# Weight preparation in a GLA slot loop: one piece a slot, or steps at eight places of the slot

## The chip, the cores and the metric

The program runs on 1 core of one Trainium2 chip. The core has five engines that work side by side: TensorE (PE in the profile, its weight loads PEld), VectorE (DVE), ScalarE (ACT), GpSimd (POOL) and SyncE (SP, which issues most of the DMAs). Each engine runs its instructions in the order in which they stand in its own queue, and waits in front of an instruction until what it needs is there. The metric is the device time of one execution in microseconds (us): 1320.1 us for the kernel before, the median of 3 runs (1319.07 to 1321.24).

## The reference

One step of a diffusion backbone with two layers. Layer 0 mixes tokens with gated linear attention (GLA), layer 1 with softmax attention. There are 256 context tokens and 1024 latent tokens of width 1024. The change touches layer 0 alone, of which this is what matters (chunks of 64 tokens, 4 heads, forward and backward in time):

```
proj = h @ w_in;  q, k, v, gate = split(proj)
logg = log_sigmoid((h @ wa1[d]) @ wa2[d] + ba[d]) / 16
for each chunk:  b = cumsum(logg);  qe = q*exp(b);  ke = k*exp(-b)
    a = tril(qe @ ke.T);  o = a @ v + qe @ S
    S = exp(b_last)*S + (k*exp(b_last - b)).T @ v
o = rms_norm(o_f + flip(o_b), onorm)
x = x + gt * ((o * silu(gate)) @ w_out)
```

The weights come in 32 bits. The kernel multiplies in 16 bits and keeps the accuracy by splitting every operand into a scaled high and a low half (three products for one).

## The kernel before

**Slots.** The GLA layer is one loop (`gla`) over 5 x 10 slots. A slot is one tile of 128 tokens of one head; there are 4 heads, and the fifth round only finishes the fourth head. In slot (h, n) the loop works on tile `order[n]`: `decayed` (L549) makes `en` and `qe` from the cumulated decay, `decay` (L525) prepares the decay of the slot after next, `value_gate` (L506) multiplies the tile with the value weights of head h and the gate weights of head h-1, `intra` (L567) makes the matrix `A` inside the tile (masked into `am` by VectorE, summed into `at` by GpSimd), `outer` (L587) and `scan` (L604) carry the state on in one direction (`Sa`, `Wa`), and `combine` (L642) and `gated` (L661) carry the other direction of the head before (`Sc`, `Wc`), add both and gate them. `local` (L628) multiplies `at` and `Sa` one slot later. So each slot is a chain that runs several times through TensorE, ScalarE, VectorE and GpSimd, and the large matrix products (L125) of `value_gate` and of the next head's q and k (`qk_piece`) stand between its links.

**Weight blocks.** A block is 1024 x 256 numbers of a weight matrix in 32 bits. `stage` (L138) loads it into one of two buffers `wst` (a DMA on SP's queue). Then a job splits it: `fill` (L179) for GLA weights, `fill_out` (L156) for the output weights, `split_ahead` (L191) for attention weights that go back to memory. A job is four reductions of 128x512 on VectorE (the block's largest value, L148 or L162), a small chain that makes a power of two of it, in which TensorE transposes once (`pow2`, L84), and four pairs of a scaled copy on ScalarE (L186, L175, L205) and a difference on VectorE (L187, L176, L206). `fold_gate` (L757) is eight multiplications of 128x256 on GpSimd (L762); it runs once, in the fifth round. The 16 matrices `wada` are loaded by SP too (L280) and used by `gemv` two slots later.

**Order.** The functions only record instructions. A scheduler then orders them for each engine, by the place where they were recorded, their dependencies and its own estimate of time; `issue_after(x)` keeps what is recorded under it behind instruction x on x's engine. In the kernel before, a staged block becomes an entry of `jobs`, and at one place of the next slot, behind `en` (`self.mark`), the whole job is recorded:

```
with self.tc.issue_after(self.mark):
    while self.jobs:
        run(self.jobs.pop(0))
```

The state of a latent sequence is loaded by SP (L614) into a single buffer `s0`, which also holds the last state on its way out (`final_state`, L624) and a row of `b_ada` (L313).

Of the kernel before, what the change touches and what calls it, by code (L numbers as in the profile page):

```python
# [52 lines left out]
class K:  # L53
# [84 lines left out]
    def stage(self, ap):  # L138
        st = self.t(self.wst, [P, KT, 256], F32, "wst")
        self.nc.sync.dma_start(st, ap.rearrange("(k p) n -> p k n", p=P))  # L140
        return st


    def scale(self, st):
        nc = self.nc
        mx = self.t(self.small, [P, 4], F32, "wmx")
        for j in range(4):
            nc.vector.tensor_reduce(  # L148
                mx[:, j : j + 1], st[:, 2 * j : 2 * j + 2, :], AX.XY, ALU.max, apply_absolute_value=True
            )  # L150
        m = self.t(self.small, [P, 1], F32, "wm1")
        nc.vector.tensor_reduce(m, mx, AX.X, ALU.max)
        return self.pow2(m)


    def fill_out(self, w, st):  # L156
        nc = self.nc
        mx = self.t(self.small, [P, 2, 2], F32, "wmx")
        par = st.rearrange("p (q b j) n -> p q b j n", q=2, j=2)
        for q in range(2):  # L160
            for b in range(2):
                nc.vector.tensor_reduce(  # L162
                    mx[:, q, b : b + 1], par[:, q, :, b, :], AX.XY, ALU.max, apply_absolute_value=True
                )
        o2 = self.onorm.unsqueeze(1).to_broadcast([P, 2, 2])
# [12 lines left out]

    def fill(self, w, j, st):  # L179
        nc = self.nc  # L180
        s, w[2][j] = self.scale(st)
        h = KT // 4
        for i in range(4):
            a, n = slice(i * h, i * h + h), slice(256 * j, 256 * j + 256)
            hi, lo = w[0][:, a, n], w[1][:, a, n]
            act = nc.scalar.activation(hi, st[:, a, :], AF.Copy, scale=s)  # L186
            dve = nc.vector.scalar_tensor_tensor(lo, st[:, a, :], s, hi, ALU.mult, ALU.subtract)  # L187
        return act.ins, dve.ins


    def split_ahead(self, name, j, st):  # L191
        nc = self.nc
        s, inv = self.scale(st)
# [6 lines left out]
        for i in range(2):  # L200
            a = slice(i * h, i * h + h)
            t = self.t(self.spl, [P, 2, h, 256], F16, "split")
            for b in range(0, h, 2):
                u, v = st[:, i * h + b : i * h + b + 2, :], slice(b, b + 2)
# [28 lines left out]
    def silu(self, x, n, tag="ls"):  # L233
# [3 lines left out]
        nc.vector.tensor_tensor(x, x, u, ALU.mult)  # L237
# [289 lines left out]
    def decay(self, h, i):  # L527
# [12 lines left out]
        nc.vector.scalar_tensor_tensor(g, u, G_SCALE, g, ALU.mult, ALU.add)  # L540
# [26 lines left out]
    def intra(self, i, st):  # L567
# [13 lines left out]
        nc.vector.copy_predicated(am, self.mask, ap)  # L581
# [21 lines left out]
    def scan(self, h, i, d, prev, u, eb, tag):  # L603
# [15 lines left out]
        if u is not None:  # L619
            w = self.t(self.ew, [P, DV], F32, "W" + tag)  # L620
            nc.vector.tensor_tensor(w, s, u, ALU.add)
# [37 lines left out]
    def gated(self, h, i, og, r, g):  # L659
        nc = self.nc  # L660
        nc.vector.scalar_tensor_tensor(g, og, r, g, ALU.mult, ALU.mult)  # L661
# [19 lines left out]
    def gla_init(self):  # L681
# [3 lines left out]
        self.v = [[None] * NT for _ in range(GH)]  # L685
        self.jobs = []

    def gla(self, wq, w, filler):
# [5 lines left out]
        for h in range(GH + 1):  # L694
# [8 lines left out]
            for n, i in enumerate(order):  # L703
# [37 lines left out]
                if h == 1 and n == 3:  # L741
                    self.fold_qk(1, wq)
# [3 lines left out]
            if h < GH:  # L746
                w = nw
# [8 lines left out]
    def fold_gate(self, gt, inv):  # L756
        nc = self.nc  # L757
        self.gt = gt
        for b in range(4):
            for i in range(2):  # L760
# [382 lines left out]
    def attention(self, wo, wk):  # L1143
# [45 lines left out]
        self.fold_gate(*self.gate_load(1), wo[0][2] + wo[1][2])  # L1189
# [49 lines left out]
def run(job):  # L1239
    return job[0](*job[1:])  # L1240
# [3 lines left out]
def emit(ctx, tc, I, O, dbg=None, stop=None):  # L1244
# [28 lines left out]
    with ExitStack() as c:  # L1273
# [98 lines left out]
        def filler(slot):  # L1372
# [30 lines left out]
            if slot == 40:  # L1403
                k.jobs.append((k.fold_gate, *k.gate_load(0), [t[2] for t in wo]))
# [6 lines left out]
            if slot in PREP:  # L1411
                n = PREP.index(slot)
                a = k.t(k.wst, [P, KT, 256], F32, "wst").rearrange("p k n -> p (k n)")[:, 0:D]
# [138 lines left out]
```

## Time and profile before

| what | value |
|---|---|
| runs of the kernel before | 1319.07, 1320.10, 1321.24 us |
| the profiled execution's own time | 1319.83 us |
| its span in the trace | 1318.1 us |
| TensorE busy | 1226.3 us (93%) |
| VectorE busy | 906.2 us (69%) |
| ScalarE busy | 713.5 us (54%) |
| GpSimd busy | 337.3 us (26%) |
| mean granted TensorE clock | 0.979 |

The slot loop lies between about 90 us and 560 us of the span: the first of its 40 rows `en` (L560) starts at 92.4 us, the last at 525.9 us, and the fifth round ends some 30 us later. After it come the output product of layer 0, layer 1 and its output. The profile shows how long each engine was busy and, for idle time, which other engine's instruction ended it. In a row of the timeline the numbers are the start, the time taken, the engine, the line, the operation and the tiles written and read, and at the end in brackets the idle time before it with what ended it.

### The profile page before, as it was taken

How to read it: one execution, taken by the hardware profiler on the slowest of the kernel's cores; microseconds unless marked ns; L12 is line 12 of the kernel's file. 1: busy time of each engine (PE TensorE's matmuls, PEld its weight loads, DVE VectorE, ACT ScalarE, POOL GpSimd, SP SyncE). 2: the span in 40 equal slices, each digit the busy share in tenths (PEclk: the TensorE clock that was granted, in tenths of full speed). 3: DMA queues.
4: the chain of work that ended last, by engine and by line, in shares of the span. 5: the costliest groups of instructions: out<-in, count | busy, mean ns of one | idle time of the engine just before them, and what ended most of it. 6: DMA issues, size and time to landing. Idle time of an engine off the chain costs nothing. (4 is left out here: it accounts for less than half of the span.)

```text
span 1318.1 us, 22427 instructions
## 1 busy us (share of the span) xinstructions
PE 1226.3 (93%) x8058; PEld 800.2 (61%) x8058; DVE 906.2 (69%) x2109; ACT 713.5 (54%) x1730; POOL 337.3 (26%) x575
## 2 busy tenths in 40 slices
PE   3799998999999998897999899999999999989997
PEld 1366665655555655674877567766665766756444
DVE  5676778776867788765765667677757677686552
ACT  2674546655656565642433476666767677673110
POOL 2132212322322243501222524232132244211000
PEclk8899998999999999998999899999999999999999
DMA  9712555545545534258444287676848748869432
GB/s 345 260 33 65 179 182 156 172 137 158 188 137 161 168 117 146 81 138 278 122 126 143 70 198 137 124 136 133 196 85 182 147 85 141 190 133 236 148 135 74
DMA packets 339487, 199.11 MB, mean 151 GB/s; under 512 B 229502, under 2 KB 325486, under 8 KB 337072
## 3 DMA queue, kind: packets, MB, share of 16 engines
q1 hardware_dynamic: 291328, 159.56, 47.4%
q10 hardware_dynamic: 47728, 37.36, 8.8%
q8 instruction: 63, 1.03, 0.3%
q0 software_dynamic: 320, 0.77, 0.3%
q14 instruction: 48, 0.39, 0.1%
HBM read 104.31 MB, written 37.24 MB: 107 GB/s over the span
## 5 line engine op out<-in xcount | busy, mean ns | idle before, releaser
L125 PEld LDWEIGHTS <-hT_hi 128*128 128x128 f16 x1920 | 189.0, 99 | 128.8 <-issue 16.3
L125 PE MATMUL mm<-whi,hT_hi 128*128 128x512 f16 (+1 forms) x576 | 200.8, 349 | 2.4 <-ACT gx L517 2.3
L125 PE MATMUL mm<-wlo,hT_hi 128*128 128x512 f16 (+1 forms) x576 | 200.7, 349 | 0.0
L125 PE MATMUL mm<-whi,hT_lo 128*128 128x512 f16 (+1 forms) x576 | 200.6, 348 | 0.0
L1085 DVE SCALAR_TENSOR_TENSOR phl<-p,srec,phl 128x1280 f16<-128x1280 f32 (+1 forms) x80 | 109.3, 1369 | 76.6 <-POOL phl L1082 43.4
L125 PEld LDWEIGHTS <-whi 128*128 128x128 f16 x1232 | 120.5, 98 | 62.8 <-issue 5.5
L125 PE MATMUL mm<-hT_hi,whi 128*128 128x256 f16 (+1 forms) x480 | 141.0, 294 | 1.9 <-DVE og L1110 1.4
L125 PE MATMUL mm<-hT_lo,whi 128*128 128x256 f16 (+1 forms) x480 | 141.0, 294 | 0.0
L125 PE MATMUL mm<-hT_hi,wlo 128*128 128x256 f16 (+1 forms) x480 | 141.0, 294 | 0.0
L125 PEld LDWEIGHTS <-hT_lo 128*128 128x128 f16 x960 | 94.4, 98 | 60.9 <-issue 2.1
L1052 PE MATMUL S<-kT,wst 128*128 128x512 f16 (+1 forms) x624 | 123.9, 341 | 7.2 <-ACT p L1060 7.2
L125 PE MATMUL mm<-PT,vh 128*128 128x256 f16 x672 | 113.8, 275 | 10.3 <-DMA PT<-phl 10.3
L1082 POOL TENSOR_SCALAR phl<-p,srec 128x1280 f16<-128x1280 f32 (+1 forms) x40 | 54.7, 1367 | 267.1 <-DVE srec L1076 132.4
L1055 DVE TENSOR_REDUCE smx<-S 128x1 f32<-128x1280 f32 (+1 forms) x80 | 101.5, 1269 | 7.6 <-PE S L1052 7.6
L1060 ACT ACTIVATE p<-S,snb,sexp 128x1280 f32<-128x1280 f32 (+1 forms) x80 | 99.3, 1242 | 7.6 <-DVE srec L1078 1.7
L1052 PEld LDWEIGHTS <-wst 128*128 128x128 f16 x624 | 61.4, 98 | 61.4 <-issue 10.3
L125 PE MATMUL mm<-PT,vl 128*128 128x256 f16 x336 | 92.3, 275 | 0.0
L148 DVE TENSOR_REDUCE wmx<-wst 128x1 f32<-128x512 f32 x104 | 64.5, 677 | 30.6 <-DMA wst<-in_gla_w_in 16.6
L125 PEld LDWEIGHTS <-vh 128*128 128x128 f16 x672 | 65.7, 99 | 21.0 <-issue 10.8
L125 PEld LDWEIGHTS <-wlo 128*128 128x128 f16 x616 | 60.3, 98 | 29.3 <-DVE wlo L1213 0.2
L1057 ACT ACTIVATE snb<-smx,nsexp 128x1 f32<-128x1 f32 x80 | 23.2, 290 | 85.4 <-DVE smx L1055 85.0
L892 POOL TENSOR_TENSOR rope<-hx,ropet 128x64 f32<-128x64 f32 x160 | 60.8, 409 | 20.3 <-ACT hx L1018 11.8
(357 smaller groups left out, 2706.0 us busy)
## 6 DMA issues: line engine op xcount, KB each, us to landing
wada<-in_w_ada SPq DMA_DIRECT2D x16, 1024.0 KB, 7.5
wst<-in_gla_w_in SPq DMA_DIRECT2D x12, 1024.0 KB, 6.4
wst<-in_att_w_in SPq DMA_DIRECT2D x10, 1024.0 KB, 7.4
og_d<-gx ACTq DMA_DIRECT2D x40, 128.0 KB, 1.8
og_d<-og ACTq DMA_DIRECT2D x40, 128.0 KB, 2.7
wst<-og_d SPq DMA_DIRECT2D x5, 1024.0 KB
xr<-x_d SPq DMA_DIRECT2D x9, 512.0 KB, 3.4
out<-xr ACTq DMA_DIRECT2D x17, 256.0 KB, 2.0
```

What stands on the lines that cost most here:

```text
L125: self.nc.tensor.matmul(out, a, b, start=k == 0 and j == 0, stop=k == n - 1 and j == 2)
L148: nc.vector.tensor_reduce(mx[:, j : j + 1], st[:, 2 * j : 2 * j + 2, :], AX.XY, ALU.max, apply_absolute_value=True)
L892: nc.gpsimd.tensor_tensor(tv[:, h, :, w, :], xv[:, h, :, 1 - w, :], sn[:, :, w, :], ALU.mult)
L1052: nc.tensor.matmul(S[:, a : a + n], x, y, start=m == 0, stop=m == 2)
L1055: last = nc.vector.tensor_reduce(mx, S, AX.X, ALU.max).ins
L1057: nc.scalar.activation(nb, mx, AF.Copy, scale=self.nsexp)
L1060: nc.scalar.activation(p, S, AF.Exp, scale=self.sexp, bias=nb, accum_out=den)
L1082: nc.gpsimd.tensor_scalar(hi, p, r, 2.0 ** 14, ALU.mult, ALU.mult)
L1085: nc.vector.scalar_tensor_tensor(lo, p, r2, hi, ALU.mult, ALU.subtract)
```

## The change

Jobs become generators: `scale`, `fill_out`, `fill`, `split_ahead` and `fold_gate` get a `yield` behind each reduction and ahead of each pair (or each pair of folds), nine steps for a block. `start` puts a job under way where it was recorded whole before. `step` records the next step of the oldest job under way, behind the chain's instruction just recorded on VectorE (`anchor`) and the TensorE instruction recorded last; it is called at eight places of a slot (five in the first round, four in the fifth). A step that needs TensorE's `pow2` waits for a place that allows it (`bank`). `room` finishes the oldest job in one piece where a buffer `wst` is needed, and `finish` all of them at a round's end and ahead of `fold_qk`.

```diff
     def stage(self, ap):
+        self.room(2)
         st = self.t(self.wst, [P, KT, 256], F32, "wst")
...
                 mx[:, j : j + 1], st[:, 2 * j : 2 * j + 2, :], AX.XY, ALU.max, apply_absolute_value=True
             )
+            yield j == 3
...
     def fill(self, w, j, st):
         nc = self.nc
-        s, w[2][j] = self.scale(st)
+        s, w[2][j] = yield from self.scale(st)
         h = KT // 4
         for i in range(4):
+            yield False
...
+    @contextmanager
+    def behind(self, ins):
+        if ins is None:
+            yield
+        else:
+            traced = self.nc.cur_bb.bb.instructions
+            pe = next(i for i in reversed(traced) if i.engine == mybir.EngineType.PE)
+            with self.tc.issue_after(ins), self.tc.issue_after(pe):
+                yield
+
+    def room(self, n):
+        with self.behind(self.mark):
+            while self.under and len(self.under) + len(self.jobs) >= n:
+                list(self.under.pop(0))
+                self.wants = None
+
+    def step(self, ins, bank=True):
+        while self.under and (bank or not self.wants):
+            with self.behind(ins):
+                self.wants = next(self.under[0], None)
+            if self.wants is not None:
+                return
+            self.under.pop(0)
...
                 if local:
                     self.local(*local)
                     local = None
+                    self.step(self.anchor)
                 if h < GH:
                     s = st[h][i] = self.decayed(h, i, g.pop(slot))
+                    self.step(self.mark, False)
                 h2, n2 = divmod(slot + 2, NT)
                 if h2 < GH:
                     g[slot + 2] = self.decay(h2, orders[h2][n2])
+                    self.step(self.anchor, False)
                 x = self.value_gate(h, i, w)
+                if h > 0:
+                    self.step(self.anchor, False)
                 if h < GH:
                     self.intra(i, s)
+                    self.step(self.anchor, h == 0)
                 if h > 0:
                     og, r, cprev = self.combine(h - 1, i, a, st[h - 1][i], cprev)
+                    self.step(self.mark if h == GH else self.anchor)
                     self.gated(h - 1, i, og, r, x)
+                    self.step(self.anchor)
...
                 with self.tc.issue_after(self.mark):
-                    while self.jobs:
-                        run(self.jobs.pop(0))
+                    self.start()
                 filler(slot)
                 if h < GH:
                     self.outer(h, i, a, s, prev, i in ends)
+                    self.step(self.anchor)
...
         for b in range(4):
+            if b:
+                yield False
             for i in range(2):
                 g = gt[:, i, 256 * b : 256 * b + 256]
                 nc.gpsimd.tensor_scalar(g, g, inv[b], 1.0, ALU.mult, ALU.mult)
```

Both programs hold the same instructions on every engine, in another order inside the loop; behind the loop the order is the same. In VectorE's order, 26 runs of four or more large rows of jobs (reductions and differences) stand unbroken in the loop before, and 16 now; rows of a job that stand alone between two rows of the chain were 11 and are 49.

VectorE, the third slot of the second round (slot 12), before. `Wc` and `Wa` are the two scans; `ks`, `g`, `ls`, `glo`, `gx` and `og` are links of the chain, `wm1` is the end of a block's maximum; `qe9` feeds TensorE's product `A` of this slot:

```order
L621 TENSOR_TENSOR Wc_598_2472<-Sc_596_2468,u9_418_1771 128x256
L152 TENSOR_REDUCE wm1_606_2492<-wmx_605_2487 128x1
L539 TENSOR_SCALAR g_627_2557<-z_625_2551,ninv_z_118_449 128x256
L229 SCALAR_TENSOR_TENSOR ls_591_2450<-gx_590_2448,ls_591_2450 128x256
L540 SCALAR_TENSOR_TENSOR g_627_2557<-ls_626_2553,g_627_2557 128x256
L621 TENSOR_TENSOR Wc_639_2613<-Sc_638_2611,u8_384_1655 128x256
L237 TENSOR_TENSOR gx_590_2448<-gx_590_2448,ls_591_2450 128x256
L621 TENSOR_TENSOR Wa_618_2531<-Sa_616_2527,U_615_2525 128x256
L545 TENSOR_TENSOR glo_629_2561<-g_627_2557,ghi_628_2560 128x256
L562 TENSOR_TENSOR qe9_581_2404<-ep_580_2401,q1_455_1923 128x256
```

VectorE at the same place now (`split` is a difference of a block, `modT1` belongs to the next layer's conditioning; the lines of the changed program are higher by 3 to 6 there):

```order
L627 TENSOR_TENSOR Wc_591_2450<-Sc_589_2446,u9_410_1744 128x256
L155 TENSOR_REDUCE wm1_598_2463<-wmx_570_2367 128x1
L212 SCALAR_TENSOR_TENSOR split_566_2351<-wst_465_1968,p2s_555_2318,split_566_2351 128x512
L580 COPY ks_628_2580<-kt_627_2577 128x256
L312 TENSOR_TENSOR modT1_39_174<-mm_646_2622,cT_34_159 128x4
L568 TENSOR_TENSOR qe9_574_2379<-ep_573_2376,q1_443_1881 128x256
L657 TENSOR_TENSOR og_593_2454<-o_592_2452,oa9_413_1752 128x256
L627 TENSOR_TENSOR Wc_632_2591<-Sc_631_2589,u8_373_1612 128x256
L545 TENSOR_SCALAR g_663_2673<-z_661_2667,ninv_z_118_449 128x256
L627 TENSOR_TENSOR Wa_610_2498<-Sa_608_2494,U_607_2492 128x256
```

Before, `Wc` and `Wa` of this slot both stand ahead of `qe9`; now only `Wc` does, and `Wa` stands four rows behind it. A block's differences, which ended ahead of `Wc`, now stand between the rows of the chain. On TensorE the product `o` that reads this `Sc` stood five large matmuls (L125, 128x512) ahead of `A` with `qe9`, and now stands 24 ahead of it.

SP's DMA queue at the same place, before (the two rows `s0` from `in_state_gla` are the loads that `Sc` and `Sa` of this slot read):

```order
L140 DMA wst_576_2388<-in_gla_w_in 128x8x256
L614 DMA s0_597_2469<-in_state_gla 128x256
L280 DMA wada_647_2632<-in_w_ada 128x8x256
L614 DMA s0_617_2528<-in_state_gla 128x256
L140 DMA wst_648_2634<-in_att_w_in 128x8x256
```

And now:

```order
L142 DMA wst_522_2211<-in_gla_w_in 128x8x256
L286 DMA wada_647_2626<-in_w_ada 128x8x256
L620 DMA s0_590_2447<-in_state_gla 128x256
L620 DMA s0_609_2495<-in_state_gla 128x256
L142 DMA wst_568_2361<-in_gla_w_in 128x8x256
```

The large load `wada` stood between the two small state loads and stands ahead of both now.

GpSimd in the last slots of the loop, before (`wst` in place is the gate's fold, `at` is the sum that `local` waits for, `ors` a small power, `Sa` and `Sc` links of the scans):

```order
L583 TENSOR_TENSOR at_6203<-am_31_149 128x128
L762 TENSOR_SCALAR wst_6554<-wst_6554,p2i_5455 128x256
L762 TENSOR_SCALAR wst_6554<-wst_6554,p2i_5755 128x256
L762 TENSOR_SCALAR wst_6554<-wst_6554,p2i_6240 128x256
L762 TENSOR_SCALAR wst_6554<-wst_6554,p2i_5455 128x256
L617 TENSOR_SCALAR Sa_6493<-Wa_6377,eb_1687_6301,eb_1715_6395 128x256
L762 TENSOR_SCALAR wst_6554<-wst_6554,p2i_5755 128x256
L762 TENSOR_SCALAR wst_6554<-wst_6554,p2i_6240 128x256
L116 TENSOR_TENSOR ors_6363<-orsa_6361,mhalf_81 128x1
L583 TENSOR_TENSOR at_6348<-am_30_148 128x128
```

And now:

```order
L589 TENSOR_TENSOR at_6323<-am_30_148 128x128
L623 TENSOR_SCALAR Sc_6595<-Wc_6539,eb_1715_6393,eb_1679_6274 128x256
L623 TENSOR_SCALAR Sc_6648<-Wc_6597,eb_1679_6274,eb_1636_6141 128x256
L117 TENSOR_TENSOR ors_6455<-orsa_6453,mhalf_81 128x1
L820 TENSOR_SCALAR wst_6554<-wst_6554,p2i_5572 128x256
L820 TENSOR_SCALAR wst_6554<-wst_6554,p2i_5863 128x256
L820 TENSOR_SCALAR wst_6554<-wst_6554,p2i_6353 128x256
L623 TENSOR_SCALAR Sc_6709<-Wc_6650,eb_1636_6141,eb_1597_6013 128x256
L589 TENSOR_TENSOR at_6442<-am_31_149 128x128
```

The last but one `at` stood behind six folds and the last behind all eight; now the last but one stands ahead of all of them, and the last behind three.

More of the change, by code (lines that the diff above doesn't have):

```diff
@@ L1 @@
-from contextlib import ExitStack
+import inspect
+from contextlib import ExitStack, contextmanager
 import concourse.bass as bass
@@ L180, in fill @@
         nc = self.nc
[L181 removed]
+        s, w[2][j] = yield from self.scale(st)
         h = KT // 4
         for i in range(4):
+            yield False
             a, n = slice(i * h, i * h + h), slice(256 * j, 256 * j + 256)
             hi, lo = w[0][:, a, n], w[1][:, a, n]
[L186 to L188 removed]
+            nc.scalar.activation(hi, st[:, a, :], AF.Copy, scale=s)
+            nc.vector.scalar_tensor_tensor(lo, st[:, a, :], s, hi, ALU.mult, ALU.subtract)
     def split_ahead(self, name, j, st):
         nc = self.nc
[L193 removed]
+        s, inv = yield from self.scale(st)
         h = KT // 2
@@ L685, in gla_init, with finish, start @@
         self.v = [[None] * NT for _ in range(GH)]
+        self.jobs, self.under, self.mark, self.wants = [], [], None, None
+    @contextmanager
[19 more added lines that the diff above has]
+            self.under.pop(0)
+    def finish(self):
+        with self.behind(self.mark):
+            for job in self.under:
+                list(job)
+        self.under, self.wants = [], None
+    def start(self):
+        for job in self.jobs:
+            r = job[0](*job[1:])
+            if inspect.isgenerator(r):
+                self.under.append(r)
         self.jobs = []
@@ L1188, in attention @@
                         self.prep = self.out2_prep(row, (first[:, 0], first[:, 1]))
-        self.fold_gate(*self.gate_load(1), wo[0][2] + wo[1][2])
+        run((self.fold_gate, *self.gate_load(1), wo[0][2] + wo[1][2]))
         wo[:] = [(hi, lo, 512) for hi, lo, _ in wo]
@@ L1239, in run @@
 def run(job):
-    return job[0](*job[1:])
+    r = job[0](*job[1:])
+    return list(r) if inspect.isgenerator(r) else r
 @with_exitstack
@@ L1403, in filler @@
             if slot == 40:
+                k.room(2)
                 k.jobs.append((k.fold_gate, *k.gate_load(0), [t[2] for t in wo]))
@@ L1412, in filler @@
                 n = PREP.index(slot)
+                k.room(1)
                 a = k.t(k.wst, [P, KT, 256], F32, "wst").rearrange("p k n -> p (k n)")[:, 0:D]
```

15 lines of the change are left out of this document (10 added, 5 removed).

## The prediction

> **What bounds the kernel now.** I read the page's first part, then the busy time by stage, then TensorE's waits in the loop, and only then the timelines around the longest of them.
>
> ```profile
> span 1318.1 us, 22427 instructions
> PE 1226.3 (93%) x8058; PEld 800.2 (61%) x8058; DVE 906.2 (69%) x2109; ACT 713.5 (54%) x1730; POOL 337.3 (26%) x575
> 90.00:560.00 470.00, 449.34 (x2774) 283.41 (x2772) 360.08 (x980) 272.70 (x715) 142.26 (x242) 0.99 0.46 144
> ```
>
> TensorE bounds the program. The third row is the slot loop (stretch, length, then busy time of PE, PEld, DVE, ACT, POOL, then the granted clock): TensorE is busy for 449.3 of 470 us, so all idle time that a better order of the other engines could give back is 20.7 us. VectorE is busy for 360.1 us there, 77%, in a fixed order, so it can hold up TensorE though it isn't full. The waits of TensorE in this stretch (who waited for whom: total, times, longest) are these:
>
> ```profile
> PE A L637 <- POOL at L583: 4.5, 4, 2.6
> PE A L578 <- DVE qe L562: 3.3, 1, 3.3
> PE mm L125 <- ACT gx L517: 2.8, 5, 0.9
> PE cs L554 <- ACT ep L558: 2.1, 1, 2.1
> PE z L649 <- POOL Sc L617: 2.0, 1, 2.0
> PE U L594 <- ACT v L513: 1.6, 2, 1.1
> PE o L649 <- DVE wm L152: 1.4, 2, 0.7
> ```
>
> Four waits are 2 us or longer (3.3, 2.6, 2.1, 2.0), and one of the four on `at` is 1.3; these five are 11.3 us, and the other 9.4 us are waits of about a microsecond or less. Long waits cost more than their length:
>
> ```profile
> 220.00:230.00 10.00, 8.31 (x28) 4.82 (x29) 9.15 (x27) 6.20 (x16) 3.37 (x7) 0.66 0.19 62
> 500.00:510.00 10.00, 9.34 (x43) 6.29 (x43) 8.43 (x27) 8.10 (x22) 3.75 (x8) 0.83 0.15 40
> 540.00:550.00 10.00, 8.99 (x58) 7.24 (x58) 7.77 (x22) 6.64 (x22) 5.24 (x7) 0.83 0.08 28
> ```
>
> The clock falls to 0.66 behind the wait of 3.3 us and to 0.83 behind those of 2.1 and of 2.6 and 2.0: 3.4, 1.7 and 1.7 us of full-speed time, 6.8 in all. So 20.7 + 6.8 = 27.5 us is the most that any order of the loop can gain: nothing under 1319.8 - 27.5 = 1292.3 us can come from here. (TensorE also waits behind the loop, but the order there is unchanged.)
>
> **The change, part by part.** No instruction is added or taken away on any engine, DMAs included, so every cost is one of order. What moves is the split of the blocks and the gate's fold:
>
> ```profile
> L148 DVE TENSOR_REDUCE wmx<-wst 128x1 f32<-128x512 f32 x92 | 57.1, 677 | 26.7 <-DMA wst<-in_gla_w_in 12.7 <-DMA wst<-in_att_w_in 7.9 <-DMA wst<-in_att_w_out 6.1
> L206 DVE SCALAR_TENSOR_TENSOR split<-wst,p2s,split 128x512 f16<-128x512 f32 x56 | 40.4, 756 | 11.7 <-ACT split L205 11.5
> L187 DVE SCALAR_TENSOR_TENSOR wlo<-wst,p2s,whi 128x512 f16<-128x512 f32 x36 | 25.8, 757 | 1.9 <-ACT whi L186 1.9
> L162 DVE TENSOR_REDUCE wmx<-wst 128x1 f32<-128x512 f32 x16 | 10.0, 674 | 0.3 <-DMA wst<-in_gla_w_out 0.3
> ```
>
> These are 133 of VectorE's 360 us, some 0.62 to 0.72 us a row in a run (57.1 / 92, 40.4 / 56); four in a run hold up the chain's next row by about 2.6 us. I go by the places where TensorE waits.
>
> *1. The wait of 3.3 us, in slot 12.*
>
> ```profile
> 212.00 0.35 SPq L614 DMA_DIRECT2D s<-in_state_gla  x1
> 212.45 0.37 SPq L280 DMA_DIRECT2D wada<-in_w_ada  x1
> 215.69 0.35 SPq L614 DMA_DIRECT2D s<-in_state_gla  x1
> 214.23 1.43 POOL L615 TENSOR_SCALAR Sc<-s,eb 128x256 f32<-128x256 f32 x1 [6.72 <-DMA s<-in_state_gla]
> 219.75 0.47 POOL L615 TENSOR_SCALAR Sa<-s,eb 128x256 f32<-128x256 f32 x1 [1.13 <-DMA s<-in_state_gla]
> 220.25 0.42 DVE L621 TENSOR_TENSOR Wa<-Sa,U 128x256 f32<-128x256 f32 x1 [1.34 <-POOL Sa L615]
> 221.03 0.61 DVE L562 TENSOR_TENSOR qe<-ep,q 128x256 f32<-128x256 f32 x1
> 221.69 1.22 PE L578 MATMUL A<-qe,en 128*128 128x128 f32 x4 [3.33 <-DVE qe L562]
> ```
>
> The first state load lands 2.2 us after its issue (212.00 to 214.23), the second 4.1 us after it (215.69 to 219.75), with the 1 MB load of `wada` issued between them. VectorE stands in `Wa` for the second one, and `qe`, which TensorE needs, is queued behind `Wa`. In the new order `qe9` stands ahead of `Wa`, so the second load no longer reaches TensorE here: -3.3 and -3.4 of the clock. What is late next is the first load: `wada` goes ahead of it, and `o` on TensorE reads its `Sc`.
>
> ```profile
> wada<-in_w_ada SPq DMA_DIRECT2D x16, 1024.0 KB, 7.5
> SPq L614 <- DMA out<-s: 12.8, 2, 6.4
> 217.09 0.38 PE L125 MATMUL mm<-whi,hT_hi 128*128 128x512 f16 x1
> 217.30 0.38 PE L125 MATMUL mm<-wlo,hT_hi 128*128 128x512 f16 x1
> ```
>
> A load right behind `wada` lands about 7.5 us on, and `Sc` takes 0.5 to 1.4 more: 8.0 to 8.9. `wada` can go once `gemv` has read its buffer; from there to `o` TensorE has 24 large matmuls, 0.21 us from start to start (5.1), and a dozen small ones, some 3 at 0.25 each (the four of `A` take 1.22): about 8 us. So `o` waits for 0 to 1 us, and up to 4 if the old state, on its way out of the same buffer, isn't gone when the 1 MB starts (the longest such wait of SP was 6.4). I take 1.7. Term: -6.7 + 1.7 = -5.0, between -6.7 and -1.
>
> The page "DMA: Bandwidth & Descriptors" of the Trainium skill, section "Queues, rings and completion order", says that each DMA engine goes round between the queues for which it has work, a packet at a time, by which a small write on ScalarE's queue would not stand behind SP's 1 MB; the wait of 6.4 us for such a write does not agree with that, and by the rule the sum below would be about 1 us lower.
>
> *2. The last slots: the fold on GpSimd.*
>
> ```profile
> 530.02 2.99 POOL L762 TENSOR_SCALAR wst<-wst,p2i 128x256 f32<-128x256 f32 x4 [2.92 <-DVE ls L229]
> 533.78 0.93 POOL L762 TENSOR_SCALAR wst<-wst,p2i 128x256 f32<-128x256 f32 x2
> 535.19 0.45 POOL L583 TENSOR_TENSOR at<-am 128x128 f32<-128x128 f32 x1
> 535.69 0.70 PE L637 MATMUL A<-v,at 128*128 128x256 f32 x2 [2.60 <-POOL at L583]
> 541.01 0.70 PE L649 MATMUL z<-Sc,qe 128*128 128x256 f32 x2 [1.95 <-POOL Sc L617]
> ```
>
> Six folds (3.9 us) delay the `at` for which TensorE waits 2.60. Now none stands ahead of this `at`, and three (2.0 us at the mean of these rows, 3.92 / 6) ahead of the next, with more matmuls of `value_gate` around it. I leave 1.2 of the 2.60. The scans' `Sc` and `Wc` still run in turn between GpSimd and VectorE, so 1.0 of the 1.95 stays, and with it half of the clock's 1.7. Term: -1.4 - 0.95 - 0.85 = -3.2, between -6.2 and +2.
>
> *3. The wait of 2.1 us at 498.6.* VectorE runs four reductions and three differences ahead of `qe` (L562) there. In the new order four of each stand ahead of `qe6`, recorded whole by `room`, and the slot behind has no large matmuls either. Term: 0, between -3.8 (wait and clock) and +2.
>
> *4. The short waits, 9.4 us.* They follow runs of job rows and the chain's own length. Runs of four or more fall from 26 to 16, which in proportion would take 3.6; but 49 single rows now stand between chain rows. I take half: -2, between -9.4 and +9.4.
>
> *5. New waits.* SP's queue carries the loads of blocks, of `wada` and of the state in a new order, and the jobs end later, so a load that waits for a `wst` buffer holds back those behind it. The nearest row is the wait of 2.1 us with its 1.7 of clock, 3.8 together; I take most of one such: +3, between 0 and +11 (three).
>
> The Trainium skill, page "TensorE: Matmul & The Clock Gate", section "Part 1: The HAM clock gate (the "warmup" mystery)", puts the fall of the clock behind about 3.4 us of idleness. The trace agrees for the wait of 3.3 us, but not for that of 2.1, behind which the clock was 0.83 over 10 us. By the rule alone a new wait of 2 us would cost 2 and the sum would be 1.7 lower.
>
> The sum: -5.0 - 3.2 + 0 - 2 + 3 = -7.2, against the profiled execution's 1319.8: 1312.6. The median of the runs is 0.3 higher, so I say 1313.
>
> **Rivals.** (a) *The blocks' own loads.* A reduction that stands alone between two chain rows waits in order for its block's landing, with the chain behind it. VectorE idled 26.7 us ahead of L148's rows already, almost all of it hidden. If the later jobs make SP issue later and as much again is added, of which half reaches TensorE, that is +13, and with -7.2 for the rest 1326. It decides from 7 us that reach TensorE on. For it: SP's loads wait for the buffers that the jobs free. Against it: `room` still finishes the older job before a new load is recorded. (b) *Nothing changes in the end*: the short waits come back at other links, since the chain of a slot is as long as before; the terms cancel to within 2.6 us, about 1320. For it speaks that no wait but those in 1 and 2 has a single cause. (c) *All runs were the cause*: terms 2 and 4 reach their lower ends and 5 is nothing: -5 - 6.2 - 7 = -18, 1302.
>
> **The numbers.** The forecast (3 to 14 us gained) has a chance of 0.48, (c) 0.12, (b) 0.14 and (a), or any other new wait that outweighs the gain, 0.26. About 0.2% (2.6 us) is what a measurement of this kernel can tell from no change. So faster 0.60, same 0.14, slower 0.26. The range runs from (c)'s 1302 to 1326 of (a).
>
> **What would show it.** If step 1 is right, the `A` of slot 12 has no wait above 1 us for `qe` and the clock stays at 1.00 from 220 to 230 us. If step 2 is right, TensorE's waits for `at` fall from 4.5 us to some 2. For (a), VectorE's idle time ahead of L150 (L148 before) would rise well above 26.7 us and TensorE's idle time in the loop above 20.7. The forecast is wrong if a wait of over 3 us for a load of state, `wada` or `wst` stands in TensorE's list.

## The result

The changed kernel takes 1334.0 us (1329.0 to 1335.5, median of 4 runs), the kernel before 1319.6 us in the same comparison: a ratio of 1.011, with a 95% interval of 1.0088 to 1.0131. It is 14.4 us slower. The forecast was 1313 us, faster.

The profiled execution took 1329.0 us, the shortest of the four. Its part behind the loop is some 7 us shorter than in the profile before, with the instructions in the same order; why is not shown. The loop itself is 15.9 us longer: TensorE's first `y` matmul behind it starts at 605.4 us instead of 589.6. The busy time by stage tells where. The stretches are cut at ScalarE's copy `gx` of slot 29 (422 us before, 423 after) and at that `y`; the columns are the stretch, its length and the busy time of PE, PEld, DVE, ACT and POOL, then the granted clock. The kernel before:

```profile
90.00:422.00 332.00, 322.25 (x2026) 201.23 (x2024) 249.28 (x671) 189.22 (x485) 91.56 (x160) 0.99 0.49 151
422.00:589.00 167.00, 156.10 (x968) 103.58 (x967) 127.83 (x350) 93.90 (x255) 52.31 (x85) 0.98 0.44 128
```

The changed kernel:

```profile
90.00:423.00 333.00, 323.45 (x2024) 199.47 (x2022) 245.26 (x651) 184.67 (x481) 84.66 (x160) 0.99 0.46 144
423.00:605.00 182.00, 161.22 (x973) 105.23 (x972) 135.64 (x372) 99.05 (x262) 52.13 (x85) 0.96 0.43 131
```

Up to slot 29 nothing is won and hardly anything lost: TensorE idles 9.6 us, as before (9.8). From there to the loop's end it idles 20.8 us instead of 10.9, and works at a lower clock (0.96 instead of 0.98). The list of TensorE's waits in the whole loop (who waited for whom: total, times, longest) is a new one:

```profile
PE A L584 <- DVE qe L568: 7.5, 3, 2.9
PE mm L126 <- ACT gx L523: 5.4, 6, 2.2
PE o L655 <- DVE p2m L89: 3.8, 5, 1.1
PE cs L655 <- DVE og L657: 2.6, 1, 2.6
PE U L600 <- ACT oa L645: 2.0, 1, 2.0
PE cs L560 <- ACT ep L564: 1.4, 2, 1.0
PE z L655 <- DVE og L657: 1.3, 1, 1.3
...
PE A L643 <- POOL at L589: 0.6, 1, 0.6
```

What stands ahead of the longest of them on VectorE is shown by its timeline at three places: `qe` is late for TensorE by 2.75 us at 519.2, by 1.82 us at 433.1, and at 465.1 a wait of 2.22 us for `gx` follows from `am`.

```profile
512.34 2.46 DVE L150 TENSOR_REDUCE wmx<-wst 128x1 f32<-128x512 f32 x4 [0.36 <-DMA wst<-in_gla_w_in]
515.21 3.01 DVE L181 SCALAR_TENSOR_TENSOR wlo<-wst,wso,whi 128x512 f16<-128x512 f32 x4
518.61 0.41 DVE L568 TENSOR_TENSOR qe<-ep,q 128x256 f32<-128x256 f32 x1
...
429.39 1.28 DVE L150 TENSOR_REDUCE wmx<-wst 128x1 f32<-128x512 f32 x2 [3.11 <-DMA wst<-in_att_w_out]
430.59 2.07 DVE L193 SCALAR_TENSOR_TENSOR wlo<-wst,p2s,whi 128x512 f16<-128x512 f32 x3
432.57 0.42 DVE L568 TENSOR_TENSOR qe<-ep,q 128x256 f32<-128x256 f32 x1
...
457.45 0.69 DVE L165 TENSOR_REDUCE wmx<-wst 128x1 f32<-128x512 f32 x1 [3.04 <-DMA wst<-in_gla_w_out]
458.06 0.44 DVE L587 COPY_PREDICATED am<-mask,A 128x256 f32<-128x256 int32 x1
```

At the first place a block that `room` records whole (four reductions) stands together with the four differences of the block before it, eight large rows ahead of `qe`. At the other two a reduction waits 3 us for its block's load with the chain queued behind it. So the steps did not take the runs away; at the first place rows of two blocks meet in one slot. That is how three of the waits come about; it is not shown that the others come about in the same way. Counted over VectorE's rows of the loop in the trace (any other row ends a run; the numbers given with the change went by another count), runs of four or more job rows fell from 24 to 16, while job rows that stand alone rose from 23 to 63, and TensorE's waits of over 0.9 us rose from 6 to 14.

### The profile page after: what moved, and what is told of

It reads as the page before. It is cut to its first block, busy times and chain, and to the rows that moved or that the text cites. A ratio compares the mean times of both kernels' runs of the same rounds, so it can differ in the third digit from the quotient of the medians.

```text
span 1327.2 us, 22429 instructions
## 1 busy us (share of the span) xinstructions
PE 1229.8 (93%) x8058; PEld 798.3 (60%) x8058; DVE 908.3 (68%) x2109; ACT 712.4 (54%) x1730; POOL 331.0 (25%) x575
## 5 line engine op out<-in xcount | busy, mean ns | idle before, releaser
L150 DVE TENSOR_REDUCE wmx<-wst 128x1 f32<-128x512 f32 x104 | 66.8, 678 | 29.9 <-DMA wst<-in_gla_w_in 16.2
```

What stands on the lines that cost most here:

```text
L150: nc.vector.tensor_reduce(mx[:, j : j + 1], st[:, 2 * j : 2 * j + 2, :], AX.XY, ALU.max, apply_absolute_value=True)
```

## The experiments

All ratios are against runs of the kernel before on the same chip. With the new functions in place but every job recorded whole, the order on every engine is that of the kernel before, row for row; so each difference below comes from steps (or from what the run adds). There is one profile to a run, so a time read from profiles alone is rough: the order of the kernel before was traced twice (the second time with the fold alone in steps, below), with the first `y` matmul at 589.6 and at 584.3 us.

**Which slots.** The jobs that start in some slots go in steps, the others are recorded whole:

```
             r = job[0](*job[1:])
             if inspect.isgenerator(r):
+                if self.slot < 29:        # second run: >= 29, third run: <= 20
                     self.under.append(r)
+                else:
+                    list(r)
```

> Jobs that start in slots 0 to 28 go in steps as in the changed kernel, those of slots 29 to 49 are recorded whole as before. Theory L (the loss lies in the late slots: in the changed kernel the gate's copy `gx` of slot 29 is 2 us behind the kernel before, that of slot 42 is 16 us behind): 1319 to 1323 us, and TensorE's first `y` matmul at 590 to 593 us. Rival S (single job rows cost about the same wherever they stand): the 34 blocks lose in proportion, so about 1328 us.

> The mirror image: whole jobs in slots 0 to 28, steps from slot 29 on (seven blocks and the gate's fold). Theory L: the loss is nearly all here, 1329 to 1334 us. Rival S: about a quarter of the loss, 1323 us. A third way: the two halves don't add up, because what is late at slot 29 decides the rest; then both this and the mirror image would stand near 1320.

> Steps for the jobs that start up to slot 20, whole jobs from slot 21 on. Theory I (steps cost nothing in themselves in the rounds that have the next head's products; what costs is that the blocks are late when the rounds without them begin, and eight slots of whole jobs make up for that): 1317 to 1321 us, with the 24th block's load back at 414 to 420 us. If steps cost the same everywhere, some 60% of what steps up to slot 28 cost (8.4 us): about 1324 us.

Measured: 1328.3 us with steps up to slot 28 (ratio 1.0064, interval 1.0043 to 1.0084), 1324.2 us with steps from slot 29 (1.0040, 1.0020 to 1.0059), 1328.2 us with steps up to slot 20 (1.0074, 1.0048 to 1.0100). Theory L falls: the early steps cost more than the late ones, though the profile shows the lost time late, and the two parts add up to about the whole (0.64% + 0.40%). By the block it is the other way round: of the 27 blocks that are split in the loop 20 start up to slot 28 and seven later (the 34 of the first expectation is a slip). Theory I falls as well: eight slots of whole jobs do not make up for the steps ahead of them. So does the rule that steps cost the same everywhere, since steps up to slot 20 cost as much as steps up to slot 28 and not 60% of it. In the profile of the third run most of the loss lies in slots 21 to 28, where jobs are whole again (`gx` is 5 us behind the kernel before in slot 20 and 15.6 in slot 28); in that of the run with steps up to slot 28 it lies from slot 30 on. So where a profile shows the wait is not where the steps were put in. But the order isn't that of the kernel before there either: with the jobs whole again, VectorE's rows still stand in another order in every slot up to the loop's end, in both runs. So these runs don't show what steps in one stretch cost by themselves.

**Which jobs.** The output weights' blocks and the fold whole, and the fold alone in steps (the condition is `job[0] not in (self.fill_out, self.fold_gate)` in the first run and `job[0] == self.fold_gate` in the second):

> Only the four blocks of the output weights (`fill_out`) and the gate's fold are recorded whole; all other blocks go in steps. If the four output blocks in steps are the cause of the late loss: 1320 to 1324 us. If it is that any block in steps is in the way in slots 30 to 39, where six blocks fall into ten slots: 1329 us or more.

> The kernel before with the gate's fold alone in steps. By the prediction's second term: TensorE's wait of 2.6 us for `at` behind the six folds goes, 1316 to 1318 us. If the wait comes back at another link: 1319 to 1321 us, with a new wait of 2 us or more behind `at` in the fifth round.

Measured: 1327.6 us (1.0066, 1.0045 to 1.0087) and 1316.5 us (0.9987, 0.9967 to 1.0007). The first lies between its two expectations: the four output blocks in steps are part of the cost, not the whole. The second says nothing of the fold. In its trace the rows of every engine and the DMAs of SP stand in the order of the kernel before (by the tiles' names, without their numbers), so six folds still stand ahead of the same `at`, and the run measured the kernel before once more; the interval of its ratio holds 1. GpSimd's timeline of the run with the fold alone in steps, and its line in TensorE's waits:

```profile
526.20 2.43 POOL L824 TENSOR_SCALAR wst<-wst,p2i 128x256 f32<-128x256 f32 x4 [3.04 <-DMA wst<-gt_d]
529.67 0.93 POOL L824 TENSOR_SCALAR wst<-wst,p2i 128x256 f32<-128x256 f32 x2
531.09 0.45 POOL L589 TENSOR_TENSOR at<-am 128x128 f32<-128x128 f32 x1
```

```profile
PE A L643 <- POOL at L589: 4.5, 5, 2.4
```

**Late blocks, or rows between the links.** A load starts at the moment when the last difference of the block two before it ends (485.0 us for both in the kernel before). In steps a job takes longer from its first reduction to its last difference (24 us instead of 19.5 in the last seven blocks), so loads start later. Theory B blames this, rival S the single rows. Four runs were made: whole jobs one slot later, two steps at each place, and a spare buffer for two late blocks, with steps and with whole jobs.

```
     def start(self):                       # one slot later; step() does nothing
+        while self.under:
+            list(self.under.pop(0))

-    def step(self, ins, bank=True):        # two steps a place
+    def step(self, ins, bank=True):
+        self.one(ins, bank)
+        self.one(ins, bank)
+    def one(self, ins, bank=True):

-    def stage(self, ap):                   # spare buffer, in slots 32 and 36
-        self.room(2)
+    def stage(self, ap, spare=False):
+        self.room(3 if spare else 2)
+        pool, tag = (self.ada, "wada") if spare else (self.wst, "wst")
```

> No steps at all: every block's job and the gate's fold are recorded whole, but one slot later than in the kernel before. Theory B (the loss comes from blocks that are late: a load starts only when the block two before it has left its buffer, and in steps it leaves later; the load of the 24th block starts at 416.5 us before and at 432.7 in the changed kernel): without any single rows the blocks are late here too, so 1326 us or more. Rival S (single job rows between the links of the chain cost the time): 1317 to 1322 us.

> The changed kernel with two steps at each place, so a job is done in half the places. Theory B: the buffers come free earlier, 1321 to 1327 us, and the last difference of a block before 552 us (559.4 in the changed kernel). Rival S: as many job rows stand among the chain's rows as before, 1330 to 1335 us.

> The changed kernel, with the blocks of slots 32 and 36 loaded into the buffer of `wada`, which is free by then, as a third buffer. Theory B: the late blocks come 8 us or more earlier and the time falls to 1321 to 1328 us. Rival S: the rows and their places are the same, 1331 to 1335 us.

> The kernel before with the same spare buffer for the blocks of slots 32 and 36. Theory B: the late blocks wait for buffers here too (each load of the last seven but one starts when an older block's last difference ends), but TensorE feels little of it: 1314 to 1319 us. Rival S: nothing changes, 1318 to 1320 us.

Measured: 1321.9 us (1.0021, 0.9998 to 1.0043); 1321.4 us (1.0016, 0.9993 to 1.0038); 1326.9 us (1.0063, 1.0042 to 1.0085); 1314.1 us (0.9961, 0.9940 to 0.9982). The first lies in the range of rival S, the other three in those of theory B, so the ranges do not decide between them. The traces say more. With whole jobs one slot later the 24th block's load starts at 426.6 us (416.5 before, 432.7 in the changed kernel): some 60% of the lateness, without steps, for 0.2% with an interval that holds zero. With two steps at a place that load starts at 434.7 us, no earlier than in the changed kernel, and nearly all of the loss is gone all the same. Both speak against theory B as the whole account.

The second run speaks against rival S as I had put it, too: the rows are as many, but only 28 stand alone (63 in the changed kernel), and runs of four are back at 25. Whether the shorter stay of its late jobs helps as well, it does not tell (some 20 us in the last seven blocks, as in the kernel before). The spare buffer helps steps by some 6 us and whole jobs by 5, so between the two remain 12.8 us: waiting for these two blocks is not what separates them. But the buffer is worth time by itself, which the kernel before left lying. In the profiles the loop is 6 us longer than before in each of the first two runs, so part of the loss in the loop may be lateness.

**The press of the late blocks.** Slots 29 and 31 without their blocks, in steps and whole (`AHEAD` loses its last two entries, and `ahead["o1"]` is set to `ahead["o0"]`, so both leave out half of the attention's output weights):

> The changed kernel without the two blocks of slots 29 and 31 (they are neither loaded nor split; the last half of the attention's output product then uses the weights of the first half). Theory P (what costs is the press of seven blocks in the slots from 29 on, with two buffers): the difference to the kernel before with the same two blocks left out falls from 15 to 5 us or less. Rival S (steps between the links of the chain): it stays at 10 us or more.

> The kernel before without the same two blocks, to compare with the run of steps above (the last half of the attention's output product uses the weights of the first half here too). VectorE has some 12 us less work in slots 29 to 33, which lies beside TensorE's: 1314 to 1319 us under both theories.

Measured: 1304.6 us in steps and 1298.4 us whole (0.9885, 0.9861 to 0.9908, and 0.9837, 0.9806 to 0.9868, of the kernel before). The difference is 6.2 us instead of 14.4: between the two expectations. With four runs each the two intervals touch, and in the two profiles the first `y` is only 2.3 us apart (586.9 and 584.6 us). So the press of blocks raises the cost of the steps; whether it is all of it these runs do not settle. Whole jobs were expected at 1314 to 1319 us and came out far below: most of what both gain against the kernel before (15 and 16 us in their profiles, from the first `y` on) lies behind the loop, so the times say little beyond their difference.

**Which rows.** First only the pairs in steps, then only the reductions, then the pairs again with ScalarE's copies recorded ahead of the differences:

```
-            yield j == 3                   # pairs in steps: reductions in one piece
+            if j == 3:
+                yield True

         for i in range(4):                 # reductions in steps: no yield in the pairs
-            yield False

         for i in range(4):                 # differences in steps
-            yield False
...
             nc.scalar.activation(w[0][:, a, n], st[:, a, :], AF.Copy, scale=s)
+        for i in range(4):
+            yield False
...
             nc.vector.scalar_tensor_tensor(lo, st[:, a, :], s, hi, ALU.mult, ALU.subtract)
```

> The four reductions of a block in one piece at the first place, the four pairs in steps as in the changed kernel. If the single reductions are what costs (each stands in VectorE's order between two links, and the power of two that TensorE and ScalarE wait for comes only behind the fourth): 1319 to 1324 us. If it is the pairs (a copy of 0.71 us on ScalarE ahead of `gx` and `oa`, a difference of 0.75 us on VectorE): 1329 to 1334 us.

> The mirror image: reductions in steps, then the power of two and all four pairs in one piece. If the single reductions cost: 1328 to 1334 us. If the pairs cost: 1319 to 1324 us. If the two add up as the early and the late slots did, each of the two runs is 5 to 9 us above the kernel before.

> As the run with the pairs alone in steps (1340 us), but ScalarE's copies are recorded ahead of the differences, two or four in a piece; only VectorE's differences go in steps. If the copies between `en` and `ep` and ahead of `gx` on ScalarE are what costs: 1320 to 1328 us. If the differences on VectorE, one ahead of a link each, are what costs: 1334 us or more.

Measured: pairs 1340.2 us (1.0160, 1.0134 to 1.0187), reductions 1322.0 us (1.0019, 1.0002 to 1.0036), differences alone 1337.9 us (1.0166, 1.0128 to 1.0203). This settles which rows cost when they alone go in steps: the differences on VectorE. Reductions in steps cost 0.2%, differences in steps 1.6% (with the pairs in steps more than the expected 1329 to 1334 us), whether ScalarE's copies go with them or not. The two do not add: with both in steps the loss is 1.1%, less than with the pairs alone. So these runs do not by themselves explain the changed kernel.

TensorE's waits say how the differences cost it. With the pairs in steps:

```profile
PE A L645 <- POOL at L591: 14.0, 11, 2.6
PE cs L562 <- ACT ep L566: 7.8, 8, 1.7
PE z L657 <- POOL Sc L625: 5.0, 2, 3.5
```

With the differences alone in steps:

```profile
PE A L653 <- POOL at L599: 13.5, 11, 2.6
PE cs L570 <- ACT ep L574: 7.4, 8, 1.5
PE z L665 <- POOL Sc L633: 4.5, 2, 2.9
```

The same waits come in both, 11 for `at` and 8 for `ep`; before, `at` cost 4.5 us in 4 waits. In the kernel before, a run of job rows that holds differences stands directly ahead of one of the rows `en`, `qe`, `am`, `gx` or `ls`, for which ScalarE, GpSimd or TensorE waits in the same slot, 14 times of 57; 43 of its differences stand ahead of `g`, which serves the slot after next, or of `ks`. With the pairs in steps it is 34 times of 70, and 8 differences are left ahead of those two. This count is no price, though: it is 24 of 57 in the changed kernel, and also 26 of 59 with the reductions in steps and 23 of 60 with two steps at a place, which cost next to nothing. And `at` itself takes longer. GpSimd's rows `at` as a group (busy time, mean ns of one, idle time ahead), before:

```profile
L583 POOL TENSOR_TENSOR at<-am 128x128 f32<-128x128 f32 x40 | 22.9, 573 | 58.8 <-DVE am L581 39.8 <-DVE wm L152 7.6 <-DVE p2e L94 5.5
```

With the pairs in steps:

```profile
L591 POOL TENSOR_TENSOR at<-am 128x128 f32<-128x128 f32 x40 | 28.2, 704 | 66.8 <-DVE am L589 62.1 <-DVE wm L156 3.1 <-DVE wm L174 1.4
```

By the timeline 15 of the 40 `at` run beside a difference on VectorE (0.15 us of overlap or more), 5 before; those take 0.86 us in the mean, and 0.46 where VectorE does nothing. The timeline of that run around its longest wait for `at`:

```profile
503.32 0.43 DVE L589 COPY_PREDICATED am<-mask,A 128x256 f32<-128x256 int32 x1
503.78 1.59 DVE L214 SCALAR_TENSOR_TENSOR split<-wst,p2s,split 128x512 f16<-128x512 f32 x2
503.84 0.99 POOL L591 TENSOR_TENSOR at<-am 128x128 f32<-128x128 f32 x1 [1.44 <-DVE wm L174]
504.88 1.22 PE L645 MATMUL A<-v,at 128*128 128x256 f32 x2 [2.63 <-POOL at L591]
```

A step recorded behind the anchor `am` puts its difference exactly beside the `at` that reads `am`. Of the 14.0 us of waits for `at` in this run that is the smaller part: seven of the 11 rows run beside a difference, and together take 2.8 us more than 0.46 each. The rest is `am` coming late or GpSimd's rows ahead of `at`; ahead of the waits of 2.5 and 2.2 us (at 539.6 and 425.1) four and two reductions, whole in this run, stand on VectorE.

In the changed kernel these waits are not there: by its list above it waits 0.6 us for `at` and 1.4 us for `ep`. At two of its three places above, differences stand in a run ahead of `qe`; how much of its loss comes from that, no run shows.

**Three buffers, and a version that beats both.** A third staging buffer for the whole loop with steps, with whole jobs, and with whole jobs and the fold in steps; and the spare buffer for two blocks with the fold in steps:

```
+        k.wst3, k.nst = k.pool("wst3", ctx=c), 0
...
+            pool = (self.wst3, self.wst, self.wst)[self.nst % 3]
+        self.room(2 if self.nst is None else 3)
+        st = self.t(pool, [P, KT, 256], F32, "wst")
...
-            st["u"] = self.t(self.tl, [P, DV], F32, f"u{i}")
+            st["u"] = self.t(self.tl, [P, DV], F16, f"u{i}")
-        st["oa"] = self.t(self.tl, [P, DV], F32, f"oa{i}")
+        st["oa"] = self.t(self.tl, [P, DV], F16, f"oa{i}")
```

> The changed kernel with a third staging buffer for the whole loop (the state terms `u` and the outputs `oa` are kept in 16 bits to make room, which leaves their order and their count as they are). If late buffers are the cause, no load waits for a block in steps any more, and this is within 5 us of the next run. If the places of the rows are the cause: 10 us or more above it.

> The kernel before with the same third staging buffer (`u` and `oa` in 16 bits as well): like the spare buffer for two blocks or better, 1308 to 1316 us, under both theories; it is there for the run with steps.

> Whole jobs, the gate's fold in steps, and three staging buffers for the whole loop (`u` and `oa` in 16 bits). If the gains of the fold (2.5 us) and of the buffers (16 us) add up: 1299 to 1302 us. If the fold's gain lay in the same waits that the third buffer takes away: 1303 us.

> The kernel before with only the gate's fold in steps and the spare buffer for the blocks of slots 32 and 36. If the two gains (2.5 and 4.9 us) touch different slots and add up: 1310 to 1313 us. If both take away the same late wait: 1314 us, like the spare buffer alone.

Measured: 1330.4 us in steps (1.0069, 1.0037 to 1.0101), 1303.1 us whole (0.9876, 0.9847 to 0.9905), 1303.6 us whole with the fold in steps (0.9890, 0.9865 to 0.9914), and 1311.6 us for the spare buffer with the fold in steps (0.9943, 0.9924 to 0.9962). With most of the waiting for loads out of the way (VectorE idles 9.6 us ahead of the loop's reductions, 30.4 in the changed kernel), steps cost 27 us, more than ever: theory B falls as the account of what steps cost. (With three blocks under way a job in steps also takes longer, over 31 us instead of 24, so this run is not a clean price.) The fold in steps is no change here either: the last two runs have the order of the same runs with a whole fold on every engine, but for two neighbouring rows of ScalarE beside the spare buffer. So they repeat those runs, 1303.6 beside 1303.1 us and 1311.6 beside 1314.1, and the expectations on adding up had nothing to add.

In the run with whole jobs and three buffers, VectorE hardly waits for blocks any more, and TensorE idles 2.6 us up to slot 29 (412 us here) instead of 9.8. The 16 bits are not it: the rows that write or read `u` and `oa` take as long as before (0.37 us on ScalarE, 0.41 to 0.44 on VectorE). But of the 17 us between the two profiles only 8.5 lie ahead of the first `y` (581.1 us); the other 9 lie behind the loop, where the order is the same, and their cause is not shown. The group of reductions, and the stretch up to slot 29:

```profile
L154 DVE TENSOR_REDUCE wmx<-wst 128x1 f32<-128x512 f32 x92 | 57.0, 675 | 1.4 <-DMA wst<-in_gla_w_in 1.4
```

```profile
90.00:412.00 322.00, 319.43 (x2031) 199.94 (x2030) 249.32 (x673) 191.37 (x488) 87.53 (x161) 1.00 0.52 162
```

The version with full 32-bit intermediates that beats both kernels is whole jobs and the spare buffer, at 1314.1 and 1311.6 us in the two runs; with `u` and `oa` in 16 bits and three buffers it is 1303.1 and 1303.6 us.

## Why the prediction was wrong

The step that failed is the one from a place to the loop: term 1 took a wait that leaves slot 12 as time won, and term 5 gave the waits that the moved rows make elsewhere one wait's price, 3 us, where they cost about 14. Term 4 had the wrong sign besides. In the profiles the long waits (1.8 us or more) with the clock behind them take 22.8 us instead of 16.8, where terms 1, 2, 3 and 5 had left 11.6; the short ones take 16.0 instead of 10.7; and some 4.5 us of the loop's 15.9 stand in TensorE's busy time, traced to no wait.

**Term 1 (slot 12, -5.0): wrong.** What it said would be seen was seen: the `A` of slot 12 has no wait for `qe`, and the clock is 1.00 from 220 to 230 us (row below). But the wait came back two slots on, 2.93 us for `qe` at 241.0 behind four reductions of the next block, with the clock at 0.83. ScalarE's `gx` is 1.8 us ahead of the kernel before in slot 10 and 0.6 us ahead in slot 17: 1.2 us lost over these slots instead of 5.0 won. The term counted what stood ahead of `qe` in one slot and not what the moved job met in the next.

**Term 2 (the fold, -3.2): the waits fell, the time was not won.** The order of the folds changed as shown, and TensorE's waits for `at` fell to 0.6 us, further than forecast. But waits of 2.6 and 1.3 us for `og` stand in the same round, with the clock at 0.66: 7.3 us with the clock, where the two waits and the clock of the kernel before were 6.2. What the folds' order is worth by itself no run shows, since the run with the fold alone in steps did not change it.

**Term 3 (0): right in the sum.** The wait of 2.1 us for `ep` is gone, and one of 2.75 us for `qe` stands one slot on, with the whole reductions of `room` ahead of it, as said; this lies inside its bounds.

**Term 4 (short waits, -2): wrong in sign, inside its bounds.** The waits below 1.8 us add up to some 16 us instead of 11. It took the broken runs for the gain and half of it for the cost of the single rows, with no row to go by. The runs with only the reductions or only the differences in steps show that it depends on the row: 0.2% for the one, 1.6% for the other.

**Term 5 (new waits, +3): mis-sized.** Six waits of 1.8 to 2.9 us stand in the changed kernel, 14.3 us together, and the falls of the clock behind them cost 8.5 us. Terms 1 to 3 had left 8.5 us of these 22.8 in place, so about 14 fall on this term, above its upper bound of 11.

**Rival (a)** had the sign, a time 8 us too short and, as a whole, the wrong cause. TensorE's idle time in the loop rose to 30 us, as it said. But VectorE's idle time ahead of L150 fell from 26.7 to 26.0 us, and with the output weights' row it rose only from 27.0 to 30.4:

```profile
L150 DVE TENSOR_REDUCE wmx<-wst 128x1 f32<-128x512 f32 x92 | 59.4, 678 | 26.0 <-DMA wst<-in_gla_w_in 12.2 <-DMA wst<-in_att_w_in 7.1 <-DMA wst<-in_att_w_out 6.6
L165 DVE TENSOR_REDUCE wmx<-wst 128x1 f32<-128x512 f32 x16 | 10.4, 679 | 4.4 <-DMA wst<-in_gla_w_out 4.4
```

Two of the three waits shown above do stand behind such a load, but taking two thirds of this waiting away (three buffers) made the steps no cheaper. The same passage of the prediction held those 26.7 us for "almost all of it hidden"; with a third buffer and whole jobs they go, and 16 us of the time with them, by the profiles half of it in the loop. **Rival (c)** came nowhere near; its -18 also takes -7 for term 4, whose lower end is -9.4.

What stays open: what makes most of the changed kernel's waits, why steps for reductions and differences together cost less than for the pairs alone, and how much of the loss in one stretch of slots follows from steps in an earlier one through the order, and how much through late loads.

The rule of the Trainium skill on the clock gate (page "TensorE: Matmul & The Clock Gate", section "Part 1: The HAM clock gate (the "warmup" mystery)"), about 3.4 us of idleness, is again not what the trace shows: the clock is below 1 in four stretches of 10 us, and no wait of TensorE in the loop is longer than 2.93 us. The changed kernel by stretches of 10 us:

```profile
220.00:230.00 10.00, 8.48 (x58) 4.99 (x56) 8.13 (x25) 4.18 (x12) 5.39 (x10) 1.00 0.78 249
240.00:250.00 10.00, 8.78 (x43) 5.01 (x44) 7.16 (x22) 4.00 (x10) 3.39 (x5) 0.83 0.24 71
500.00:510.00 10.00, 10.00 (x47) 5.69 (x46) 6.59 (x19) 6.00 (x19) 1.84 (x3) 0.83 0.51 148
520.00:530.00 10.00, 9.41 (x43) 5.99 (x42) 8.78 (x27) 6.83 (x19) 5.06 (x9) 0.83 0.36 121
560.00:570.00 10.00, 7.92 (x33) 5.24 (x34) 6.32 (x21) 5.71 (x20) 4.69 (x8) 0.66 0.30 93
```

## What to carry to other kernels

Before background work is cut into pieces, look at what each piece would stand ahead of: a run of rows ahead of one link that has slack can be cheaper than the same rows spread one by one ahead of links that have none. Price the kinds of rows apart, since here the reductions were nearly free in steps and the differences were not. Look at the order in the trace before reading a run as a test of an order: three runs here were recorded in another way and left the order as it was, but for two rows in one of them. And when each load starts exactly as an older buffer comes free and its reader then waits two microseconds again and again (14 times in this loop), count that as time that may be won until a run with one more buffer says otherwise.

## What the runs showed of the hardware

By the profile, whose spans on GpSimd are rough, a row of GpSimd takes about twice as long in the mean beside a difference on VectorE (two inputs from SBUF). In the kernel before, the state's `Sc` (L617) takes 0.55 us where VectorE does nothing and 1.34 us in the mean beside a difference (7 of 32 rows); the masked sum `at` takes 0.46 and 0.86 us in the run with the pairs in steps. Beside a reduction, which has one input, `Sc` takes 0.55 us (one row), and 0.56 with the pairs in steps (three rows). The Trainium skill, page "SBUF — State Buffer", section "Who interferes with whom", says that a VectorE instruction with two SBUF inputs contends with a GpSimd instruction that reads SBUF, and that the pair of ports they share is an exclusive lock. These durations agree with it, and they make the place behind `am` a bad one for a difference.
